# The last expert's output stays on chip: one-hot matmuls in place of its scatter-add to DRAM

## The chip, the cores and the metric

The kernel runs on one core of a Trainium2 chip. The core has TensorE (PE: matmuls and transposes, with its weight loads shown apart as PEld), VectorE (DVE), ScalarE (ACT), GpSimd (POOL), and SyncE (SP), which issues most of the DMAs. SBUF is the memory on the core, PSUM the memory that matmuls write to, DRAM lies outside. The metric is the device time of one execution in microseconds (us), as the median of several runs.

## The reference

One decoder layer over 512 tokens of width 1024, in float32. What matters here is its last third:

```
h = h + concat([ret, att]) @ w_out[i]
h = h + moe(rmsnorm(h, g_moe_norm[i]), ...)          # 32 experts, each token goes to 4
gate = jax.nn.sigmoid(h @ w_ple_gate[i])
h = h + rmsnorm(gate * (p[i] @ w_ple_proj[i]), g_ple_norm[i])
return rmsnorm(h, g_final)
```

In `moe`, a token's result is the sum over its four experts of (gate weight) x (expert output). An expert is an up projection to 2 x 1024 columns, a clamped SwiGLU, and a down projection to 1024 columns. The stage after it, called the epilogue below, multiplies `h` by `w_ple_gate` and needs the whole sum over the experts.

## The kernel before

**Sums in DRAM.** A DRAM tensor `acc` (512 x 1024) is first filled with the residual stream. The experts run one after another, sorted by their number of tokens. For each, POOL gathers its tokens' rows, PE runs the up and down projections, ACT multiplies the rows by the gate weights into a tile `y` (`gated`, line 928), and POOL adds them to `acc` with an indirect DMA that reads, adds and writes (`scatter`, line 933). After the last expert SP loads `acc` back in four tiles of 128 tokens, `h2[0]` to `h2[3]` (line 1165).

**Two kinds of experts.** The twenty larger ones (`BIG`, up to 96 rows) run on operands split into a high and a low part, three products each; the splits are lines 150 (ACT) and 151 (DVE). The twelve smaller ones (up to 64 rows) run in full float32 on unsplit weights; `pairs64` (line 861) computes two column halves side by side, so the output of such an expert is 128 x 512: rows 0 to 63 hold columns 0 to 511 of its up to 64 tokens, rows 64 to 127 the other columns of the same tokens. The last expert (number 31 in the order of work) is a small one.

**Buffers.** Weights arrive in 1 MB pieces in twelve tiles named `raw`. `raw_tile()` takes one, `free` lists those to be had, and `prefetch()` loads the next piece into one. Late in the kernel the same tiles serve other ends: `tmp` holds the input `p`, four halves of two tiles are `h2`, four of two others `proj`.

**Order of work at the end.** The code runs loop passes `e` = 0 to 32. Pass `e` does the up projection of expert `e` and the down projection of expert `e` - 1. At `e` = 31 a tile `last` is taken and left unused, and the activations of expert 31 are transposed (`act_t64`) before the down projection of expert 30. At `e` = 32 come the load and split of `p`, the loads of `w_ple_proj` and half of `w_ple_gate` (held back by a small ACT copy that reads the `y` of expert 30, line 221), the down projection of expert 31, its `gated` and its `scatter`. Then `project(0)` to `project(2)` multiply `p` by `w_ple_proj` for three of the four token tiles.

**A branch.** Line 1107 is a `tc.If` on whether an expert has more tokens than fit its rows. Each engine reads the flag and branches by itself; here the body is skipped. After the branch each engine waits until the work that it issued before is done, and then raises its semaphores by what the body would have added. The body uses most of PSUM, so the first PSUM users behind it wait for ACT's raise.

**Epilogue.** For each token tile `i`, `transposed(i)` (line 1176) transposes `h2[i]` on PE and splits it on ACT and DVE into `hh` and `hl`; `gate(i, c)` runs 24 matmuls for each column half `c`, a sigmoid and a sum of squares; `finish(i)` normalizes, adds and writes the output. They are called as transposed 0, project 3, gate 0 0, transposed 1, gate 1 0, gate 0 1, finish 0, gate 1 1, finish 1, and then transposed, two gates and finish for tiles 2 and 3.

**Who orders the instructions.** A scheduler orders the instructions of each engine by their place in the code and by when it computes them to be ready; an engine works through its list strictly in turn. So a later piece of code may stand earlier in an engine's list where the scheduler saw a gap.

Of the kernel before, what the change touches and what calls it, by code (L numbers as in the profile page):

```python
# [95 lines left out]
def hymba_kernel(ctx, tc, x, p, positions, rel_bias_table, g_mix_norm, w_in, b_in, ret_norm_g,  # L96
# [40 lines left out]
    def raw_tile(dt=F32):  # L137
        pl_ = free.pop(0)
        return pl_.tile([P, 2048], dt, name="raw"), pl_
# [77 lines left out]
    def prefetch(after=None):  # L217
        if free and state["next"] < min(len(pieces), state["limit"]):
            t, pl_ = raw_tile()
            if after is not None:  # L220
                nc.scalar.activation(t[:, 0:1], after[:, 0:1], AF.Copy)
            pieces[state["next"]](t)
            queue.append((t, pl_))
            state["next"] += 1

    def next_piece(parts=None, dst=None, more=True):
        t, pl_ = queue.pop(0)
        r = split(t, parts, dst)
        free.append(pl_)
        if more:  # L230
            prefetch()
        return r
# [590 lines left out]
    def act_t64(a):  # L823
        return transposed64(a, R.sb.tile([P, KD, 64], F32, name="aT64", bufs=1), 1.0 / ALPHA)
# [88 lines left out]
    def down(aT, piece, e):  # L913
        o = R.dn.tile([P, D], F32, name="dn")
        with tc.issue_after(R.up_end.ins):
            add_bias([o[:, 0:512], o[:, 512:D]], e, 1024, 512, start=True, stop=False)
        for f in range(4):
            wh, wl = piece(f)
            for kk in range(2):
                k = f * 2 + kk  # L920
                for a, w in ((aT[0], wh), (aT[1], wh), (aT[0], wl)):
                    for n in range(2):
                        nc.tensor.matmul(o[:, n * 512:(n + 1) * 512], lhsT=a[:, k, :],  # L923
                                         rhs=w[:, kk * 1024 + n * 512:kk * 1024 + (n + 1) * 512],
                                         start=False, stop=(k == KD - 1 and w is wl))
        return o

    def gated(o, gate):
        y = R.sb.tile([P, D], F32, name="y")
        nc.scalar.activation(y[:, 0:o.shape[1]], o, AF.Copy, scale=gate)  # L930
        return y

# [108 lines left out]
    with tc.issue_after(R.prep.ins):  # L1041
        ahead.append(next_piece())
    aT = None
    for e in range(E + 1):
        if e < E:
            def piece(k, e=e):
                if ahead:
                    return ahead.pop(0)
                with tc.issue_after(R.act.ins) if (e, k) == (1, 2) else nullcontext():
                    return next_piece()  # L1050

            if 0 < e < E - 2:
                static_gather(e + 2)
            h = up(xT, piece, e) if BIG[e] else up64(xT, e)
            a = act(h)
            if e == 0:
                read_slots()
                static_gather(2)
            if e + 1 < E:
                xT = (prep if BIG[e + 1] else prep64)(xe[(e + 1) % 2])  # L1060
        if e == E - 1:

            last = raw_tile()
            aT_last = act_t64(a)
        if e == E:
            tmp = raw_tile()
            p_sb = tmp[0][:, 0:D].rearrange("p (i d) -> p i d", i=NT)
            nc.sync.dma_start(out=p_sb, in_=p.rearrange("(i p) d -> p i d", p=P))
            state["limit"] = n_moe + 3
            for _ in range(3):  # L1070
                prefetch(after=y)
            ph, pl = halves(raw_tile(F32R)[0], 2)
            for i in range(NT):
                split_t(R.tp, p_sb[:, i, :], ph[:, :, i * P:(i + 1) * P], pl[:, :, i * P:(i + 1) * P], n=2)
            aT = aT_last
        if e > 0:
            big = BIG[e - 1]
            y = gated(down(aT, lambda f: next_piece(), e - 1) if big else down64(aT, e - 1), routes[e - 1][1])
            scatter(y, routes[e - 1][0], CAP if big else P, 1 if big else 2)
        if e < E - 1:  # L1080
            aT = act_t(a) if BIG[e] else act_t64(a)

    h2 = [t for _ in range(2) for t in raw_tile()[0].rearrange("p (a n) -> a p n", a=2)]
    proj = [t for _ in range(2) for t in raw_tile()[0].rearrange("p (a n) -> a p n", a=2)]
    state["limit"] = len(pieces)
    w_pr, *ws = [next_piece(more=False) for _ in range(3)]
# [20 lines left out]
    with tc.If(any_v > 0), ExitStack() as sx:  # L1107
# [9 lines left out]
        with tc.For_i(0, E, 1) as ev:  # L1117
# [4 lines left out]
            with tc.For_i(0, n_e, 1):  # L1122
# [33 lines left out]
                od = up_tile()  # L1156
                product(od, aTd, w_down, b_down, False)
                scatter(gated(od, gate), idx, P)


    ep2 = pool(ctx, "ep2", 2)
    mm = pool(ctx, "mm_e", 1, PSUM)
    tp = pool(ctx, "tp_e", 2, PSUM)
    for i in range(NT):
        ld = nc.sync.dma_start(out=h2[i], in_=acc[i * P:(i + 1) * P, :])
    with tc.issue_after(ld.ins):
        for _ in range(2):
            prefetch()
    g_ple = bcast(ep2, g_ple_norm[0], D, "g_ple", nc.sync)
    g_fin = bcast(ep2, g_final, D, "g_fin", nc.sync)  # L1170
    ws = [ws]
    free += [t[1] for t in (last, tmp, tf, tr)]
    hT = {}
    ss1 = {}

    def transposed(i):
        hT[i] = ep2.tile([P, KD, P], F32R, name="hh"), ep2.tile([P, KD, P], F32R, name="hl")
        split_t(tp, h2[i], *hT[i])

# [86 lines left out]
```

## Time and profile before

| | us |
|---|---|
| median of 3 runs | 1499.07 (1497.57 to 1502.2) |
| the profiled execution | 1498.92 |
| its span, first to last instruction | 1496.8 |
| PE busy | 1364.4 |
| DVE busy | 886.2 |
| ACT busy | 728.4 |
| POOL busy | 224.7 |

Busy times overlap, so they don't add up to the span. The profile shows the profiled execution alone, and its clock starts at the span's start. All that the change touches lies after 1335 us.

### The profile page before, as it was taken

How to read it: one execution, taken by the hardware profiler on the slowest of the kernel's cores; microseconds unless marked ns; L12 is line 12 of the kernel's file. 1: busy time of each engine (PE TensorE's matmuls, PEld its weight loads, DVE VectorE, ACT ScalarE, POOL GpSimd, SP SyncE). 2: the span in 40 equal slices, each digit the busy share in tenths (PEclk: the TensorE clock that was granted, in tenths of full speed). 3: DMA queues.
4: the chain of work that ended last, by engine and by line, in shares of the span. 5: the costliest groups of instructions: out<-in, count | busy, mean ns of one | idle time of the engine just before them, and what ended most of it. 6: DMA issues, size and time to landing. Idle time of an engine off the chain costs nothing. (4 is left out here: it accounts for less than half of the span.)

```text
span 1496.8 us, 17238 instructions
## 1 busy us (share of the span) xinstructions
PE 1364.4 (91%) x6208; PEld 939.3 (63%) x6209; DVE 886.2 (59%) x1052; ACT 728.4 (49%) x782; POOL 224.7 (15%) x230
## 2 busy tenths in 40 slices
PE   5998999588999999999999999999999999999785
PEld 4776777466676647656566647656567547675464
DVE  6635674767575627656466627656466627685256
ACT  5333543455464626544454626545455626664343
POOL 1203231472011100010100000010100100000023
PEclk9998999888999999999999999999999999999898
DMA  8432027677899999999999999999999999996601
GB/s 263 129 96 57 35 105 274 234 267 255 328 390 404 387 408 397 407 376 388 399 398 377 384 403 399 407 350 389 395 396 375 379 393 410 406 355 248 223 24 48
DMA packets 110428, 462.49 MB, mean 309 GB/s; under 512 B 10954, under 2 KB 29304, under 8 KB 77568
## 3 DMA queue, kind: packets, MB, share of 16 engines
q1 hardware_dynamic: 99584, 436.24, 74.5%
q0 software_dynamic: 10320, 24.51, 6.4%
q8 instruction: 50, 0.82, 0.2%
q10 hardware_dynamic: 432, 0.57, 0.1%
q14 instruction: 42, 0.34, 0.1%
HBM read 447.53 MB, written 18.99 MB: 312 GB/s over the span
## 5 line engine op out<-in xcount | busy, mean ns | idle before, releaser
L151 DVE TENSOR_TENSOR wl<-raw,wh 128x2048 fp32r<-128x2048 f32 (+2 forms) x267 | 584.1, 2229 | 125.2 <-ACT wh L150 124.3
L150 ACT ACTIVATE wh<-raw 128x2048 fp32r<-128x2048 f32 (+2 forms) x267 | 489.2, 1864 | 109.4 <-PE up L844 70.7
L844 PE MATMUL up<-wh,xTh 128*128 128x512 f32 x640 | 179.8, 403 | 13.1 <-ACT wh L150 11.6
L844 PE MATMUL up<-wl,xTh 128*128 128x512 f32 x640 | 179.3, 402 | 2.5 <-DVE wl L151 2.5
L844 PE MATMUL up<-wh,xTl 128*128 128x512 f32 x640 | 178.8, 401 | 0.9 <-DVE xTl L292 0.9
L861 PE MATMUL up<-raw,xTh 128*64 128x512 f32 x768 | 168.3, 594 | 0.0
L891 DVE TENSOR_SCALAR a<-up 128x512 f32<-128x512 f32 x52 | 34.0, 686 | 224.1 <-ACT sg L890 224.1
L844 PEld LDWEIGHTS up<-wh,xTh 128*128 128x128 f32 x640 | 120.4, 191 | 47.3 <-ACT wh L150 17.2
L844 PEld LDWEIGHTS up<-wl,xTh 128*128 128x128 f32 x640 | 120.7, 191 | 37.1 <-DVE wl L151 8.9
L844 PEld LDWEIGHTS up<-wh,xTl 128*128 128x128 f32 x640 | 121.7, 191 | 30.7 <-DVE xTl L292 1.6
L935 POOL DMA_INDIRECT acc<-y,slot_i x30 | 45.2, 1506 | 569.1 <-ACT y L930 497.4
L861 PEld LDWEIGHTS up<-raw,xTh 128*64 128x64 f32 x768 | 53.7, 137 | 104.6 <-issue 100.6
L923 PE MATMUL dn<-wl,aTh 128*128 128x512 f32 x320 | 102.6, 402 | 6.0 <-DVE wl L151 6.0
L890 ACT ACTIVATE sg<-up 128x512 f32<-128x512 f32 x52 | 28.9, 598 | 162.7 <-issue 148.2
L923 PE MATMUL dn<-wh,aTh 128*128 128x512 f32 x320 | 104.7, 409 | 0.1
L923 PE MATMUL dn<-wh,aTl 128*128 128x512 f32 x320 | 102.2, 401 | 0.0
L800 POOL DMA_INDIRECT xe<-xg,slot_i x30 | 42.9, 1429 | 370.8 <-PE tp L814 222.1
L861 PE MATMUL dn<-raw,aT 128*64 128x512 f32 x384 | 88.3, 598 | 0.0
L930 ACT ACTIVATE y<-dn,slots 128x1024 f32<-128x1024 f32 (+1 forms) x30 | 28.3, 944 | 102.7 <-PE dn L923 84.6
L923 PEld LDWEIGHTS dn<-wl,aTh 128*128 128x128 f32 x320 | 59.1, 189 | 22.8 <-DVE wl L151 10.0
L923 PEld LDWEIGHTS dn<-wh,aTl 128*128 128x128 f32 x320 | 61.2, 191 | 14.9
L923 PEld LDWEIGHTS dn<-wh,aTh 128*128 128x128 f32 x320 | 59.0, 191 | 17.3 <-ACT xTh L815 1.8
(338 smaller groups left out, 1577.2 us busy)
## 6 DMA issues: line engine op xcount, KB each, us to landing
raw<-in_w_up_dram SPq DMA_DIRECT2D x256, 1024.0 KB, 13.0
raw<-in_w_down_dram SPq DMA_DIRECT2D x128, 1024.0 KB, 12.3
raw<-in_w_in_dram SPq DMA_DIRECT2D x32, 256.0 KB, 4.9
raw<-in_w_out_dram SPq DMA_DIRECT2D x4, 1024.0 KB, 5.3
raw<-in_w_ple_gate_dram SPq DMA_DIRECT2D x4, 1024.0 KB, 11.4
raw<-in_w_in_dram SPq DMA_DIRECT2D x3, 1024.0 KB, 5.7
xt<-in_x_dram SPq DMA_DIRECT2D x4, 512.0 KB, 6.5
h<-in_x_dram POOLq DMA_DIRECT2D x4, 512.0 KB, 7.5
```

The costliest lines, as they stand in the source:

```text
L150: R.split_act = nc.scalar.activation(to(wh), src(raw), AF.Copy)
L151: R.split_dve = nc.vector.tensor_tensor(out=to(wl), in0=src(raw), in1=to(wh).bitcast(F32), op=ALU.subtract)
L800: return nc.gpsimd.indirect_dma_start(out=dst[0:n, 0:D // h], out_offset=None, in_=xg.rearrange("s (h d) -> (s h) d", h=h), in_offset=bass ...
L844: nc.tensor.matmul(h[n // 2][:, n % 2 * 512:n % 2 * 512 + 512], lhsT=a[:, k, :], rhs=w[:, n * 512:(n + 1) * 512], start=(k == 0 and a is x ...
L861: R.pair = nc.tensor.matmul(o[v * 64:v * 64 + 64, c:c + 512], lhsT=xT[:, k, :], rhs=w[:, v * n + c:v * n + c + 512], start=False, stop=las ...
L890: nc.scalar.activation(sg[:, cs], hv[:, :, 0], AF.Silu, scale=ALPHA)
L891: nc.vector.tensor_scalar(a[:, cs], hv[:, :, 1], LIMIT + 1.0, 1.0 - LIMIT, op0=ALU.min, op1=ALU.max)
L923: nc.tensor.matmul(o[:, n * 512:(n + 1) * 512], lhsT=a[:, k, :], rhs=w[:, kk * 1024 + n * 512:kk * 1024 + (n + 1) * 512], start=False, sto ...
L930: nc.scalar.activation(y[:, 0:o.shape[1]], o, AF.Copy, scale=gate)
L935: nc.gpsimd.indirect_dma_start(out=acc.rearrange("s (h d) -> (s h) d", h=h), out_offset=bass.IndirectOffsetOnAxis(ap=idx[0:n, :], axis=0), ...
```

## The change

The scatter of expert 31 is dropped. Its gated output `y` is written to a free part of `tmp`, and the read-back of `acc` (now `load_sums`) is issued before the down projection of expert 31, behind the scatter of expert 30. DVE builds a one-hot matrix `hot[:, i, :]` for each token tile: row r has a one in the column of the token to which row r of the expert belongs. `transposed(i)` then first multiplies this matrix with `y`, in two float32 matmuls of 64 rows (one for each column half), and DVE adds each product to `h2[i]` in place. `act_t64` of expert 31 now comes after the down projection of expert 30, `last` is gone, and the body of the `If`, which may add to `acc`, loads the sums again at its end.

```diff
-    def gated(o, gate):
-        y = R.sb.tile([P, D], F32, name="y")
+    def gated(o, gate, y=None):
+        if y is None:
+            y = R.sb.tile([P, D], F32, name="y")
         nc.scalar.activation(y[:, 0:o.shape[1]], o, AF.Copy, scale=gate)
         return y
...
+    def load_sums():
+        for i in range(NT):
+            R.sums = nc.sync.dma_start(out=h2[i], in_=acc[i * P:(i + 1) * P, :])
...
-        if e == E - 1:
-
-            last = raw_tile()
-            aT_last = act_t64(a)
...
-            aT = aT_last
+            h2 = [t for _ in range(2) for t in raw_tile()[0].rearrange("p (a n) -> a p n", a=2)]
+            load_sums()
+            hot = tmp[0][:, D:D + S].rearrange("p (i s) -> p i s", i=NT)
+            tok = small.tile([P, NT, 1], F32, name="tok", bufs=1)
+            r = RANK[E - 1]
+            nc.vector.tensor_scalar(tok, vb[:, :, 0:1], -1.0, slots[:, r, 0:1], op0=ALU.mult, op1=ALU.add)
+            for i in range(NT):
+                nc.vector.tensor_scalar(hot[:, i, :], iota, FAR, tok[:, i, :], op0=ALU.add, op1=ALU.is_equal)
         if e > 0:
             big = BIG[e - 1]
-            y = gated(down(aT, ...) if big else down64(aT, e - 1), routes[e - 1][1])
-            scatter(y, routes[e - 1][0], CAP if big else P, 1 if big else 2)
-        if e < E - 1:
+            y = gated(down(aT, ...) if big else down64(aT, e - 1), routes[e - 1][1],
+                      tmp[0][:, D + S:2 * D] if e == E else None)
+            if e < E:
+                scatter(y, routes[e - 1][0], CAP if big else P, 1 if big else 2)
+        if e < E:
             aT = act_t(a) if BIG[e] else act_t64(a)
-    h2 = [t for _ in range(2) for t in raw_tile()[0].rearrange("p (a n) -> a p n", a=2)]
...
                 scatter(gated(od, gate), idx, P)          # the last line of the If's body
+        load_sums()
...
-    for i in range(NT):
-        ld = nc.sync.dma_start(out=h2[i], in_=acc[i * P:(i + 1) * P, :])
-    with tc.issue_after(ld.ins):
-        for _ in range(2):
-            prefetch()
+    for _ in range(2):
+        prefetch()
...
     def transposed(i):
+        for v in range(2):
+            ps = mm.tile([P, 512], F32, name="mm", bufs=4)
+            rows, cs = slice(v * 64, v * 64 + 64), slice(v * 512, (v + 1) * 512)
+            nc.tensor.matmul(ps, lhsT=hot[rows, i, :], rhs=y[rows, :], start=True, stop=True)
+            nc.vector.tensor_tensor(out=h2[i][:, cs], in0=ps, in1=h2[i][:, cs], op=ALU.add)
         hT[i] = ep2.tile([P, KD, P], F32R, name="hh"), ep2.tile([P, KD, P], F32R, name="hl")
         split_t(tp, h2[i], *hT[i])
```

## Rows read from the trace of the kernel before

**Rows 1.** The page, part 1: busy us, share of the span, instructions.

```profile
PE 1364.4 (91%) x6208; PEld 939.3 (63%) x6209; DVE 886.2 (59%) x1052; ACT 728.4 (49%) x782; POOL 224.7 (15%) x230
```

**Rows 2.** Windows: length, busy us by engine, then PE clock, DMA share, GB/s.

```profile
1389.30:1400.10 10.80, 9.66 (x41) 3.41 (x41) 0.76 (x2) 2.66 (x7) 1.42 (x1) 1.00 0.74 247
...
1412.50:1418.85 6.35, 0.00 (x0) 0.00 (x1) 0.00 (x0) 1.02 (x1) 0.00 (x0) 0.76 0.98 358
1418.85:1425.20 6.35, 5.62 (x21) 4.39 (x21) 0.03 (x1) 1.57 (x3) 0.00 (x0) 0.71 0.68 261
...
1455.16:1460.20 5.04, 5.04 (x12) 3.98 (x13) 4.74 (x18) 1.52 (x5) 1.27 (x1) 0.51 0.27 104
```

**Rows 3.** Timeline of PE: start, duration, [idle before it <- what ended that].

```profile
1412.07 0.39 PE L309 MATMUL up<-wl,raw 128*128 128x512 f32 x1
1418.85 0.79 PE L307 MATMUL dn<-wh,raw 128*128 128x512 f32 x1 [6.39 <-ACTq L1107]
...
1423.43 1.03 PE L300 MATMUL tp<-cst,raw 128*128 128x128 f32 x8
1425.19 0.50 PE L307 MATMUL mm<-wh,hh 128*128 128x512 f32 x1 [0.73 <-ACT hh L291]
1425.91 0.50 PE L308 MATMUL mm<-wh,hl 128*128 128x512 f32 x1 [0.22 <-DVE hl L292]
...
1452.94 0.93 PE L307 MATMUL mm<-wh,hh 128*128 128x512 f32 x2 [1.83 <-ACT hh L291]
1455.16 0.80 PE L308 MATMUL mm<-wh,hl 128*128 128x512 f32 x1 [1.29 <-DVE hl L292]
```

**Rows 4.** Line 1107, the branch: count, duration ns, first and last start.

```profile
L1107 DVEq EVENT_SEMAPHORE  x2: 21/21/21, 1409.4 to 1409.5; - x2
...
L1107 ACTq EVENT_SEMAPHORE  x2: 17/17/17, 1418.8 to 1418.9; - x2
...
L1107 DVEq COMPARE_BRANCH  x1: 72/72/72, 1406.9 to 1406.9; - x1
...
L1107 ACTq COMPARE_BRANCH  x1: 50/50/50, 1413.0 to 1413.0; - x1
```

**Rows 5.** Instructions on `acc`, 1380 to 1440 us, and issue to landing.

```profile
L1165 SPq DMA_DIRECT2D raw<-acc x4: 345/386/807, 1406.4 to 1408.4; - x4
L935 POOL DMA_INDIRECT acc<-y,slot_i x2: 1416/1483/1550, 1390.7 to 1400.5; - x2
...
DMA to landing us min/median/max: 3.6/6.0/8.4
```

**Rows 6.** Timeline of PE, float32 matmuls of 64 rows in the attention.

```profile
139.74 2.09 PE L482 MATMUL s_ps<-akT,aqT 64*128 64x256 f32 x8
141.76 0.79 PE L315 MATMUL mm<-wh,act_l 128*128 128x512 f32 x1
...
142.60 1.13 PE L482 MATMUL s_ps<-akT,aqT 64*128 64x256 f32 x4
143.66 0.73 PE L315 MATMUL mm<-wh,act_l 128*128 128x512 f32 x2
```

**Rows 7.** Timeline of PE: 64-row bias matmuls between matmuls of 128 rows.

```profile
1344.99 1.10 PE L844 MATMUL up<-wl,xTh 128*128 128x512 f32 x4
1346.02 0.74 PE L831 MATMUL up<-bias,sel 64*128 64x512 f32 x4
1346.59 0.40 PE L831 MATMUL dn<-bias,sel 64*128 64x512 f32 x2
1346.92 0.74 PE L923 MATMUL dn<-wh,aTh 128*128 128x512 f32 x2
```

**Rows 8.** Line 751, a DVE addition of PSUM to SBUF in place.

```profile
L751 DVE TENSOR_TENSOR h<-mm,h x4: 691/692/692, 228.6 to 274.4; 128x512 f32<-128x512 f32 x4
```

**Rows 9.** Timeline of DVE at the third token tile.

```profile
1453.76 0.68 DVE L1192 TENSOR_TENSOR raw<-raw,sig 128x512 f32<-128x512 f32 x1
```

**Rows 10.** Timeline of PE at the start of expert 30's down projection.

```profile
1378.65 0.73 PE L923 MATMUL dn<-wl,aTh 128*128 128x512 f32 x2 [1.02 <-DVE wl L151]
```

More of the change, by code (lines that the diff above doesn't have):

```diff
@@ L1074, in hymba_kernel @@
                 split_t(R.tp, p_sb[:, i, :], ph[:, :, i * P:(i + 1) * P], pl[:, :, i * P:(i + 1) * P], n=2)
-            aT = aT_last
+            h2 = [t for _ in range(2) for t in raw_tile()[0].rearrange("p (a n) -> a p n", a=2)]
[6 more added lines that the diff above has]
+                nc.vector.tensor_scalar(hot[:, i, :], iota, FAR, tok[:, i, :], op0=ALU.add, op1=ALU.is_equal)
         if e > 0:
             big = BIG[e - 1]
-            y = gated(down(aT, lambda f: next_piece(), e - 1) if big else down64(aT, e - 1), routes[e - 1][1])
-            scatter(y, routes[e - 1][0], CAP if big else P, 1 if big else 2)
-        if e < E - 1:
+            y = gated(down(aT, lambda f: next_piece(), e - 1) if big else down64(aT, e - 1), routes[e - 1][1],
+                      tmp[0][:, D + S:2 * D] if e == E else None)
+            if e < E:
+                scatter(y, routes[e - 1][0], CAP if big else P, 1 if big else 2)
+        if e < E:
             aT = act_t(a) if BIG[e] else act_t64(a)
-    h2 = [t for _ in range(2) for t in raw_tile()[0].rearrange("p (a n) -> a p n", a=2)]
     proj = [t for _ in range(2) for t in raw_tile()[0].rearrange("p (a n) -> a p n", a=2)]
@@ L1171, in hymba_kernel @@
     ws = [ws]
-    free += [t[1] for t in (last, tmp, tf, tr)]
+    free += [t[1] for t in (tf, tr)]
     hT = {}
```

## The prediction

> **What bounds the kernel now.** I first read the page: PE is busy for 1364.4 of 1496.8 us [rows 1], so PE sets the pace and the question is where it stands idle. The change is confined to the end, so next I read PE's timeline there, then the instructions on `acc`, and last the branch. The reader should see three things.
>
> First, what PE waits for after the down projection of expert 31. It goes on with `project(0)` to `project(2)`, which need no expert's output, until 1412.07 + 0.39 = 1412.46. Then it idles for 6.39 us, and ACT's branch ends that idle time, no DMA [rows 3]. It then runs `project(3)`, which also needs no expert, and the first transposes of `h2` start at 1423.43 [rows 3].
>
> Second, where the scatter and the read-back stand against that. The scatter of expert 31 is issued at 1400.5, the four loads from 1406.4 to 1408.4, and none of these DMAs takes over 8.4 us from issue to landing [rows 5]. So the last tile is there by 1408.4 + 8.4 = 1416.8 at the latest, 6.6 us before even the first tile is touched, and 2 us before ACT lets PE go at all.
>
> Third, ACT's branch itself. It executes at 1413.0 in 0.05 us, but ACT's next instruction comes at 1418.8, 5.8 us later [rows 4]. In this stretch the DMA engines are 0.98 busy with the read-back and two weight loads [rows 2]. DVE's branch came at 1406.9 and its next instruction at 1409.4 [rows 4]: 2.5 us at most, for it also finished a split meanwhile. [...]
>
> **The change part by part.** The sum is made against the profiled execution, 1498.92 us, which stands 0.15 us below the median of 1499.07; I add the result to the median.
>
> *Scatter removed, read-back moved ahead: 0.* Both are covered by `project` and the branch, as above. From the issue of the scatter to the last landing they take 1416.8 - 1400.5 = 16.3 us; were ACT's branch free and PE at `h2` 5 us earlier, at 1418.4, the cover would still hold. The loads now wait on SP for expert 30's scatter, issued at 1390.7 and landed at most 8.4 us later, at 1399.1 [rows 5]. Behind them in SP's list stand SP's branch, then two loads of `w_ple_gate` and the two norm vectors. Those weights are used after two gates have run, some 20 us after the branch, so I cost that queue at nothing.
>
> *The branch: -1.1.* [...] Below: DVE's 2.5 in place of 5.8, a gain of 3.3. Above: 0, the DMA engines being full already. I take a third of the gain, since about half of the traffic goes and its moment is uncertain.
>
> [...]
>
> *The transposes of expert 31 moved behind expert 30's down projection: 0.* In front of it they gave nothing away, because that projection then waits for a DVE split anyway, 1.02 us at 1378.65 [rows 10]; that wait also swallows what is saved. Behind it they may cost their own time, half of the 1.03 us that eight transposes take [rows 3]. Bounds 0 and +0.5.
>
> *Building the one-hot matrices: 0.* Five small DVE instructions; from 1389.3 to 1400.1 DVE is busy for 0.76 of 10.8 us [rows 2]. Without that cover they would cost at most five times an addition of 512 columns, 3.5 us [rows 8].
>
> *Two float32 matmuls per token tile: 1.6 us a tile.* The trace has no such matmul of 64 x 512. The nearest are those of line 482, 64 x 256. A float32 matmul shows as two instructions; four of them go from 142.60 to 143.66 at full clock [rows 6]; less 0.2 us for the change of shape (below) that is 0.215 each, and 0.43 for twice the columns. Two matmuls are four instructions: 1.72 us end to end. If the two, which use different halves of the array's rows, run fully side by side, it is 0.86. That they can: eight instructions from 139.74 to 141.76 [rows 6] are two such streams, in 2.02 us at half clock where one by one they would need 3.4. Here the instructions come in pairs of one half, so only the inner two can overlap: three steps, 1.29. To it I add the change between 64 and 128 rows: the four from 1344.99 on follow each other at (1.10 - 0.40) / 3 = 0.233, the first bias matmul comes 0.10 late, and the six of them, in three pairs, take 0.20 more than three such steps [rows 7]. Together 0.3, so 1.6 (bounds 0.86 and 2.0).
>
> [...]
>
> *Two additions per tile on DVE: 0.69 us each* [rows 8]. They stand between matmul and transposes. The first half of the tile is added some 0.2 us after its matmul (the handing over from DVE to PE at 1425.91 has this size [rows 3]), so it is ready at 0.86 + 0.2 + 0.69 = 1.75 us while PE is done at 1.29: 0.45 idle. The second half is ready 0.69 later, four transposes take 0.5: 0.2 more. So 0.65 us of PE idle where nothing fills it.
>
> Now tile by tile. *Tile 0:* `project(3)` is ready and fills the wait, and it can also fill the 0.73 + 0.22 us that PE now waits after the transposes [rows 3]: 1.6 - 0.95 = +0.65. The half clock after the branch (0.71 on average, [rows 2]) strikes the new work instead of `project(3)`, so it costs nothing twice. *Tile 1:* 1.6 + 0.65 = +2.25. *Tile 2:* PE already idles 1.83 + 1.29 us here [rows 3], because `hl` stands behind `finish(0)` and line 1192 [rows 9] in DVE's list; the matmuls fit into that, but two more additions come ahead of `hl`: +1.4. *Tile 3:* +2.25. Sum 6.55; with the branch 5.45. That gives 1499.07 + 5.45 = **1504.5 us**. Tiles at 0.86 and 2.0 us, the moved transposes and the branch at their ends give +1.0 and +8.3 (the idle terms kept, tile 2 unchanged).
>
> **The rivals.** About 0.3%, 4.5 us, is what a measurement of this kernel can tell from no change: 1494.6 to 1503.6.
>
> *A, the forecast:* the new instructions stand in PE's list where the code has them.
>
> *B, pulled ahead.* The one-hot matmuls need neither `h2` nor the weights, so the scheduler may put tile 1's beside tile 0's, and tile 3's into PE's idle 3.1 us at tile 2. Then tile 1 costs 1.6, tile 3 nothing: 0.65 + 1.6 + 1.4 - 1.1 = +2.55, **1501.6**. For it: such fillings are how the lists are made. Against it: in the scheduler's reckoning PE may have no gap there.
>
> [...]
>
> [...]
>
> [...]
>
> **How the numbers follow.** A 0.43, of which 0.08 end below 1503.6; B 0.31; C 0.16, of which 0.10 end below 1494.6; D 0.10. Faster 0.10; same 0.08 + 0.31 + 0.06 = 0.45; slower 0.35 + 0.10 = 0.45. The time is A's. The range, 1496 to 1510, leaves out D and 0.10 of C; A's own is 1500 to 1507.4.
>
> **What would show it.** Right: the read-back is issued near 1399 and PE still stands idle until ACT's branch; each tile has four float32 instructions of 64 rows in 1.3 us at full clock; PE idles under a microsecond before the transposes of tiles 1 and 3. Wrong: PE ends `project(2)` well before 1412, or ACT's branch is over well before 1417; either moves all that follows. The forecast also falls if the clock stays full at tile 2.

## The result and the profile after

| | before | after |
|---|---|---|
| median of the runs timed together, us | 1502.16 | 1510.59 |
| ratio, 95% interval | | 1.0056 [1.0041, 1.007] |
| the profiled execution, us | 1498.92 | 1510.74 |
| its span, us | 1496.8 | 1509.0 |

The change makes the kernel 8.4 us (0.56%) slower. The forecast was slower by 5.45 us, and its range ended at 1510: the direction is right, the size too small, the time just beyond the range. Of the 6.1 us between the forecast of 1504.5 and the 1510.59, 3.1 are the median of the kernel before, 1502.16 here and 1499.07 in the forecast, and 3.0 are the change. One of the six executions of after took 4702.75 us, and the ratio leaves it out. Page of after, part 1 (the answer to [rows 1]):

```profile
PE 1374.1 (91%) x6224; PEld 942.5 (62%) x6225; DVE 892.1 (59%) x1065; ACT 729.3 (48%) x782; POOL 224.0 (15%) x229
```

PE has 16 instructions more, and is busy 9.7 us longer. Up to the end of expert 30 the changed part of the kernel has not begun to matter to PE, and yet the profile of after is already 3.5 us late there; such a shift appears between any two executions (the same point lies between 1389.4 and 1396.3 in the runs of this study). So from here on I compare the **stretch** from expert 31's first bias matmul (1390.44 before, 1393.91 after) to the end of the span: 106.4 us before, 115.1 after, +8.7. That is the measured loss (8.4 by the medians). A stretch is that of one execution; how well it repeats can be seen in e2 below, which differs from before by one scatter that costs nothing: each of its five windows agrees with the one below within 0.1 us. A ratio also holds what varies ahead of the stretch, so the two need not agree: in e7 the stretch is 3.8 us longer than before, and the ratio stands for 1.0.

The windows view cuts the stretch at the last matmul of four gates: up to the end of `gate(0, 0)`; tile 1 (to `gate(1, 1)`); tile 2; tile 3; and what comes after PE's last matmul. Columns: length, then busy us of PE, PEld, DVE, ACT and POOL, then PE's granted clock, DMA share, GB/s. Before:

```profile
1390.44:1431.54 41.10, 31.22 (x123) 20.16 (x124) 9.49 (x9) 12.74 (x17) 2.97 (x2) 0.88 0.64 217
1431.54:1450.23 18.69, 18.16 (x83) 14.37 (x81) 10.54 (x17) 9.82 (x14) 3.82 (x3) 1.00 0.00 0
1450.23:1468.39 18.16, 15.04 (x59) 11.47 (x57) 12.78 (x37) 7.61 (x18) 7.62 (x6) 0.81 0.15 59
1468.39:1481.47 13.08, 12.67 (x81) 10.94 (x78) 9.82 (x26) 5.89 (x14) 4.19 (x4) 1.00 0.07 26
1481.47:1496.83 15.36, 0.00 (x1) 0.00 (x0) 8.58 (x24) 3.39 (x10) 4.86 (x5) 0.58 0.12 46
```

After, the same five cuts:

```profile
1393.91:1436.48 42.57, 33.47 (x127) 21.06 (x127) 15.37 (x13) 17.74 (x20) 1.42 (x1) 0.84 0.60 205
1436.48:1456.73 20.25, 19.33 (x87) 14.58 (x86) 7.60 (x18) 4.99 (x11) 3.88 (x3) 1.00 0.00 0
1456.73:1479.28 22.55, 18.95 (x64) 12.93 (x63) 14.25 (x40) 7.72 (x18) 7.58 (x6) 0.77 0.12 47
1479.28:1494.46 15.18, 14.05 (x82) 11.35 (x82) 11.05 (x27) 5.99 (x14) 5.05 (x4) 1.00 0.09 35
1494.46:1508.98 14.52, 0.00 (x1) 0.00 (x0) 7.70 (x24) 3.40 (x10) 3.98 (x5) 0.62 0.10 37
```

Half of the loss, 22.55 - 18.16 = 4.39 us, lies at tile 2, and 3.9 of those are PE *busy* longer, not idle longer. Over the four windows with gates PE is busy 2.25 + 1.17 + 3.91 + 1.38 = 8.71 us longer, as much as the stretch grows. Read that with the clock beside it: 0.77 over the window. PE's timeline of after tells what is in it:

```profile
1421.83 2.08 PE L1189 MATMUL mm<-raw 64*128 64x512 f32 x4 [5.79 <-ACTq L1118]
1424.68 1.11 PE L300 MATMUL tp<-cst,raw 128*128 128x128 f32 x4 [0.78 <-DVE raw L1190]
...
1436.41 1.13 PE L1189 MATMUL mm<-raw 64*128 64x512 f32 x4
1438.32 1.25 PE L300 MATMUL tp<-cst,raw 128*128 128x128 f32 x8 [0.78 <-DVE raw L1190]
...
1456.66 1.13 PE L1189 MATMUL mm<-raw 64*128 64x512 f32 x4
1461.39 1.97 PE L300 MATMUL tp<-cst,raw 128*128 128x128 f32 x8 [3.60 <-DVE raw L1190]
1463.19 1.22 PE L307 MATMUL mm<-wh,hh 128*128 128x512 f32 x2
1464.35 2.07 PE L1189 MATMUL mm<-raw 64*128 64x512 f32 x2
...
1479.20 1.12 PE L1189 MATMUL mm<-raw 64*128 64x512 f32 x2
1480.26 0.66 PE L300 MATMUL tp<-cst,raw 128*128 128x128 f32 x4
```

Four groups of one-hot matmuls were expected, and there are five. Tile 3's were split: two of its four instructions stand inside the first gate of tile 2 (1464.35), where PE runs at half clock (0.50 in the windows below), and take 2.07 us instead of 1.12. Ahead of tile 2's transposes PE waits 3.60 us for the addition on DVE. DVE's timeline shows why it is late:

```profile
1458.19 0.67 DVE L254 SCALAR_TENSOR_TENSOR rs_v<-ss_f 128x1 f32<-128x1 f32 x1 [0.79 <-ACT raw L1224]
...
1459.99 0.68 DVE L1206 TENSOR_TENSOR raw<-raw,sig 128x512 f32<-128x512 f32 x1
1460.60 0.14 DVE L271 TENSOR_SCALAR rs_t<-rs_t 128x1 f32<-128x1 f32 x1
1460.66 0.68 DVE L1190 TENSOR_TENSOR raw<-mm,raw 128x512 f32<-128x512 f32 x1
```

The product is there at 1457.8, but the addition stands behind the second half of `finish(0)` (line 254 and what follows) and a `sig` multiplication. PE's clock behind the two long waits, in windows of after (columns as above):

```profile
1421.91:1425.91 4.00, 3.22 (x9) 1.65 (x10) 1.29 (x2) 0.08 (x1) 0.00 (x0) 0.50 0.70 242
1425.91:1429.91 4.00, 4.00 (x13) 3.18 (x13) 2.34 (x2) 2.81 (x3) 0.00 (x0) 0.53 0.08 27
1461.91:1465.91 4.00, 4.00 (x11) 2.05 (x9) 3.19 (x13) 1.80 (x3) 0.86 (x1) 0.50 0.16 62
1465.91:1469.91 4.00, 4.00 (x9) 2.81 (x9) 2.71 (x7) 1.24 (x4) 0.44 (x1) 0.50 0.19 73
1469.91:1473.91 4.00, 4.00 (x17) 3.24 (x16) 3.35 (x10) 0.15 (x2) 2.09 (x2) 0.91 0.00 0
```

Busy time times (1 - clock) is my estimate of what the clock cost: 1.6 + 1.9 = 3.5 behind the branch and 2.0 + 2.0 + 0.4 = 4.4 behind tile 2, 7.9 us. Before, the same product from [rows 2] is 5.62 x 0.29 + 5.04 x 0.49 = 4.1. So by this estimate about 3.8 of the 8.71 us are the clock. The other 4.9 are about what the one-hot matmuls of four tiles take with the change of shape (1.1 to 1.3 us a tile, worked out below).

Of the things that were to change nothing, two lines. The branch (now line 1118; the answer to [rows 4]) and the read-back (now line 1048; to [rows 5]):

```profile
L1118 ACTq EVENT_SEMAPHORE  x2: 17/17/17, 1421.8 to 1421.8; - x2
...
L1118 ACTq COMPARE_BRANCH  x1: 50/50/50, 1416.6 to 1416.6; - x1
```

```profile
L1048 SPq DMA_DIRECT2D raw<-acc x4: 339/400/429, 1402.5 to 1403.8; - x4
```

The read-back is issued at 1402.5, 3.5 us of shift beyond the 1399 that was forecast. ACT's branch takes 5.2 us in place of 5.8, with the DMA engines busy for 0.65 of it and no longer 0.99. The difference tells little: with the read-back moved, ACT's branch takes 5.4 us in e1, 4.0 in e7 and 5.3 in e12. The prediction's -1.1 us for the branch takes it that less traffic on the DMA engines shortens it. DVE's next instruction comes 2.5 us behind its branch in both kernels, with the DMA engines busy for 0.70 of it before and for the whole of it after; a split on DVE fills 2.43 and 2.50 us of that, so the branch by itself can't be read there. That traffic sets the length of the branch is not shown.

### The profile page after: what moved, and what is told of

Its sections match the earlier page's. It is cut to its first block, busy times and chain, and to the rows that moved or that the text cites. A ratio compares the mean times of both kernels' runs of the same rounds, so it can differ in the third digit from the quotient of the medians.

```text
span 1509.0 us, 17281 instructions
## 1 busy us (share of the span) xinstructions
PE 1374.1 (91%) x6224; PEld 942.5 (62%) x6225; DVE 892.1 (59%) x1065; ACT 729.3 (48%) x782; POOL 224.0 (15%) x229
## 5 line engine op out<-in xcount | busy, mean ns | idle before, releaser
L150 ACT ACTIVATE wh<-raw 128x2048 fp32r<-128x2048 f32 (+2 forms) x267 | 489.7, 1865 | 108.4 <-PE up L844 67.0
L923 PE MATMUL dn<-wh,aTh 128*128 128x512 f32 x320 | 104.3, 407 | 0.1
```

The lines of the kernel that those rows point to most:

```text
L150: R.split_act = nc.scalar.activation(to(wh), src(raw), AF.Copy)
```

## The experiments

Sixteen kernels. "Stretch" is that of the profiled execution of each; ratios are to the kernel before. The computation is left incomplete in e1, e2, e3, e10, e11 and e16: there the last expert's rows, or those of some tiles, are missing.

### What moving the read-back gives, without the one-hot work

**e1** leaves the five lines of the one-hot loop out of `transposed`, **e2** is the kernel before less one scatter:

```diff
 # e1, in after's transposed(i)
-        for v in range(2):
-            ps = mm.tile([P, 512], F32, name="mm", bufs=4)
-            ...
 # e2, in before
-            scatter(y, ...)
+            if e < E:
+                scatter(y, ...)
```

> The changed kernel without the one-hot matmuls and the additions (the last expert's output is left out of the sum); the earlier read-back and all else stay. Read: ratio to before, and the stretch from the first bias matmul of expert 31's down projection to the end (before 106.4 us, changed 115.1). Theory 'work in the epilogue': all that was lost is the one-hot work, so the stretch falls back to 105 to 107 and the ratio is 1.000 within 0.002. Rival 'moved read-back': the loads now stand ahead of the branch in SP's list and delay what follows; then the stretch stays above 112 and the ratio above 1.003.

Measured: 0.9965 [0.9951, 0.9979], stretch 101.0: below what either theory had.

> The kernel before without expert 31's scatter (its output is left out of the sum), the read-back where it was. Theory 'hidden': the scatter stands beside project and ACT's branch, so the stretch stays at 106.4 within 1 us and the ratio is 1.000 within 0.002. Rival 'scatter on the path': the stretch falls by the 4.5 us that the scatter took to land, or more, and the ratio is below 0.998.

Measured: 0.9996 [0.9987, 1.0006], stretch 106.4. The scatter and its cover are as forecast: worth nothing. But e1, where the scatter is gone, the read-back moved and the one-hot work left out, is 5.4 us shorter than before. A part of the cause is in its PE timeline:

```profile
1416.41 1.07 PE L300 MATMUL tp<-cst,raw 128*128 128x128 f32 x8 [0.45 <-PEq L1118]
1421.97 0.80 PE L307 MATMUL dn<-wh,raw 128*128 128x512 f32 x1 [4.50 <-ACTq L1118]
```

The transposes of tile 0 now stand ahead of `project(3)` in PE's list and run while PE would only wait for ACT's branch; before, they came behind it [rows 3]. No transfer got shorter on the path: an *order* changed, and the window up to `gate(0, 0)` fell from 41.10 to 38.72. And tile 2 took 15.64 us instead of 18.16:

```profile
1450.73:1466.37 15.64, 12.57 (x58) 9.76 (x57) 12.44 (x36) 7.59 (x18) 7.39 (x6) 1.00 0.10 38
```

PE's idle time there is the same as before, 3.07 against 3.12 us; the clock stayed at 1.00, where it was 0.81.

**e6** is the kernel before, with that order alone:

```diff
+    with tc.issue_after(R.tr.ins):          # R.tr: the last transpose
         project(mm.tile([P, D], F32, name="dn"), (3,))
```

> The kernel before with one change: PE's transposes of token tile 0 are put ahead of project(3) in PE's list; scatter, read-back and all else stay. Theory 'the gain of the first experiment is a place in PE's list': the transposes need no PSUM of the branch's body, so they run while ACT branches, and the stretch falls from 106.4 to 103.5 to 104.6 with the scatter still in place. Rival 'the gain comes from the missing scatter and the earlier read-back': the stretch stays at 106 to 107.

Measured: 0.9986 [0.9976, 0.9996], stretch 104.0. PE's timeline of e6 has the transposes where e1 has them:

```profile
1416.79 1.06 PE L300 MATMUL tp<-cst,raw 128*128 128x128 f32 x8 [0.45 <-PEq L1107]
```

The order by itself gives 2.4 us, without any of the change. e1 has 3 us more: 1.55 of it is tile 2 again, which took 17.19 us here at a clock of 0.90, and 1.44 is tile 1 (19.62 us against 18.18). This order explains neither.

### What the one-hot work costs, by kind and by tile

After against e1: 115.1 - 101.0 = 14.1 us, where the prediction's terms sum to 6.55. **e11** keeps the matmuls and drops the additions; **e10**, **e3** and **e16** leave the one-hot loop out for tile 0, tile 2, and tiles 1 and 3:

```diff
 # e11
-            nc.vector.tensor_tensor(out=h2[i][:, cs], in0=ps, in1=h2[i][:, cs], op=ALU.add)
 # e10, e3, e16
-        for v in range(2):
+        for v in range(2 if i != 0 else 0):      # e3: i != 2;  e16: i % 2 == 0
```

> The kernel after with all its one-hot matmuls, but none of the additions: the products stay unused in PSUM and the last expert's rows are missing from the sums. Theory (the matmuls cost their own 1.1 to 1.6 us a tile and hold tile 0's transposes behind ACT's branch; the rest of the 14.1 us is the additions, for which PE waits and behind which the splits queue): stretch 106 to 108, in place of 115.1 with the additions and 101.0 without either. Rival (it is the matmuls: the change of shape and the half clock that follows): stretch 112 to 115, ratio over 1.003.

Measured: 1.0012 [1.0001, 1.0024], stretch 109.0: between the two theories. The matmuls, with what they hold up, are 8.0 of the 14.1 us, the additions 6.1.

> The kernel after without the one-hot matmuls and the additions of token tile 0 (the last expert's rows are missing from that tile's sums); tiles 1 to 3 keep theirs. Theory (tile 0's matmuls need PSUM that the body of the If uses, so they and the transposes behind them can't run under ACT's branch; without them the transposes run there and the branch hides them): the first gate matmul comes at 33 us of the stretch in place of 36.8, and the stretch falls from 115.1 to 110.5 to 112. Rival (a tile costs its matmuls and one wait for its addition, wherever it stands): first gate matmul at 34.5 to 35.5, stretch 112.7 to 113.7.

Measured: 1.0006 [0.9995, 1.0016], stretch 108.8. First half right: tile 0's transposes are under ACT's branch again, 0.45 us behind PE's own as in e1, and the first gate matmul comes at 32.9 us of the stretch. The stretch fell by 6.3, more than either theory said: up to tile 2 the gain is 3.9, and then tile 2, whose code is that of after, takes 19.80 us in place of 22.55:

```profile
1450.56:1470.36 19.80, 16.22 (x64) 11.38 (x63) 14.16 (x39) 7.83 (x18) 7.59 (x6) 0.91 0.14 54
```

Same wait (3.58), same instructions; PE's clock came back earlier, 0.91 on average against 0.77. Tile 3's pair stands in the first gate of tile 2 here too, and most of it runs at full clock (0.60 from 1457.75 to 1458.75, then 1.00):

```profile
1458.15 1.30 PE L1189 MATMUL mm<-raw 64*128 64x512 f32 x2
```

> The changed kernel without the matmuls and additions of token tile 2 alone (that tile lacks the last expert's output). Theory 'DVE queue': tile 2 costs 4.4 of the 8.7 us, since its additions stand behind the work of finish(0) on DVE; the stretch falls from 115.1 to about 110.7. Rival 'each tile costs its matmuls': tile 2 costs what tiles 0, 1 and 3 do, about 2, and the stretch is about 113.

Measured: 1.0006 [0.9994, 1.0017], stretch 109.4, tile 2 16.96 us long. The stretch fell by 5.7 us, more than the theory's 4.4 and far from the rival's 2.

> The kernel after without the one-hot matmuls and additions of token tiles 1 and 3 (the last expert's rows are missing from those tiles); tiles 0 and 2 keep theirs. Theory (these two tiles cost what the milestones of the new kernel show, 1.5 and 2.1 us): the stretch falls from 115.1 to 111 to 112, ratio 1.0025 to 1.0035. The prediction's terms (2.25 each) give 110.6. Rival (leaving out any tile also reorders what stands behind it, as leaving out tile 0 gave 6.3 us): stretch 107 to 109.5, ratio under 1.0015.

Measured: 1.0015 [1.0003, 1.0028], stretch 108.4: the rival, though not for its reason. Tiles 1 and 3 give back 2.06 and 2.11 in their own windows, almost what the prediction had. The rest is at tile 2:

```profile
1454.63:1473.69 19.06, 15.38 (x62) 11.11 (x63) 13.56 (x38) 7.87 (x18) 7.58 (x6) 0.91 0.15 56
```

The wait of 3.59 us is still there and tile 2's own matmuls too; what is gone is tile 3's pair in the middle of the half-clock stretch, and 22.55 - 19.06 = 3.5 us with it. The pair alone need not be the cause, for e10 has it in the same place and is 2.75 us shorter than after at tile 2. By busy time times (1 - clock) the low clock at tile 2 costs 18.95 x 0.23 = 4.4 us in after, 1.5 in e10 and 1.4 in e16: by this estimate some 3 us of either gain are the clock.

So single tiles give back 6.3 (0), 5.7 (2) and 6.6 (1 and 3), 18.6 in all where the sum is 14.1: each also shortens the half clock behind tile 2 (mean clock of that window 0.91, 0.90 and 0.91, against 0.77), and that can be gained only once.

### Moving the additions, and moving what waits for them

**e4** and **e5** call `transposed(2)` ahead of `finish(0)`, and no longer behind `finish(1)`, in after and in before:

```diff
     gate(0, 1)
+    transposed(2)
     finish(0)
...
-        transposed(i)
+        if i > 2:
+            transposed(i)
```

> The changed kernel with transposed(2) (its matmuls, additions, transposes and splits) called ahead of finish(0) instead of after finish(1); nothing is left out. Theory 'DVE queue': PE's 3.6 us wait for tile 2's additions shrinks to the 0.8 of tile 1, and the slow clock after it goes too; the stretch falls by 5 to 8 us, to 107 to 110. Rival 'each tile costs its matmuls': only PE's amount of work counts, and the stretch stays at 114 to 116.

Measured: 1.0018 [1.0008, 1.0028], stretch 110.3. The wait at tile 2 fell to 0.29, and the next one appeared:

```profile
1476.36 1.97 PE L300 MATMUL tp<-cst,raw 128*128 128x128 f32 x8 [4.45 <-DVE raw L1190]
```

Tile 3's addition now stands behind `finish(1)`.

> The kernel before with transposed(2) called ahead of finish(0); nothing is left out. Theory 'tile 2 is bound by the order on ACT and DVE': PE's waits of 1.83 and 1.29 us at tile 2 and the slow clock after them go, and the stretch from expert 31's first bias matmul to the end falls from 106.4 to 101 to 103, ratio 0.996 to 0.998. Rival 'DVE has too much to do': the work of finish is only pushed back and meets the end; stretch 105 or more.

Measured: 0.9983 [0.9974, 0.9993], stretch 104.3: the same in the kernel before, tile 2 without idle time and then 4.64 us for `hh` at tile 3.

**e7** puts all eight additions ahead of the branch (and once more at the end of its body), **e8** is e7 with `transposed(2)` early, **e12** puts tiles 0 and 1 there and tiles 2 and 3 behind `transposed(1)` and `gate(1, 0)`, and calls `transposed(2)` and `transposed(3)` ahead of the two finishes:

```diff
+    def add_last(i, ps):                 # e12; e7 and e8: all four tiles in one loop
+        for v in range(2):
+            rows, cs = slice(v * 64, v * 64 + 64), slice(v * 512, (v + 1) * 512)
+            nc.tensor.matmul(ps[v], lhsT=hot[rows, i, :], rhs=y[rows, :], start=True, stop=True)
+            nc.vector.tensor_tensor(out=h2[i][:, cs], in0=ps[v], in1=h2[i][:, cs], op=ALU.add)
+    ...                                  # called ahead of the If, into up_tile()
     any_v = nc.values_load(any_blk[0:1, 0:1], min_val=0, max_val=NT)
```

> The changed kernel with the one-hot matmuls and additions of all four tiles issued ahead of the branch, behind project(2), and repeated in its body; the split of the last weights is kept behind the branch. Nothing is left out. Theory 'cover': PE idles 5.8 us and DVE 11 us there, so the eight matmuls (4.5 us) and eight additions (5.5 us) hide, and the stretch falls from 115.1 to 101 to 104, below the 106.4 of before; ratio 0.996 to 0.999. Rival 'DVE's own branch': the additions hold it back, PE waits for it in turn, and the stretch stays at 106 to 109.

Measured: 1.0007 [0.9997, 1.0016], stretch 110.2. The rival's mechanism held, a little beyond its range of 106 to 109. In e7's PE timeline and its branch lines:

```profile
1424.88 1.97 PE L300 MATMUL tp<-cst,raw 128*128 128x128 f32 x8 [3.60 <-DVEq L1128]
```

```profile
L1128 DVEq EVENT_SEMAPHORE  x2: 21/21/21, 1424.8 to 1424.9; - x2
...
L1128 DVEq COMPARE_BRANCH  x1: 72/72/72, 1421.9 to 1421.9; - x1
```

DVE reaches its branch only at 1421.9, behind the additions, and PE waits for DVE's branch instead of ACT's.

> The kernel of the run before (additions ahead of the branch) and transposed(2) called ahead of finish(0). If both theories hold the two gains add: stretch 96 to 100, ratio 0.993 to 0.996. If tile 2's gain is only pushed back, it is that of the run before.

Measured: 1.0006 [0.9995, 1.0018], stretch 109.4; it is e7 with the wait of 4.87 us moved to tile 3.

> The kernel after with its one-hot additions moved: those of tiles 0 and 1 ahead of the branch, beside the projections (and once more in the skipped body), those of tiles 2 and 3 behind the transposes of tile 1 and the first gate of tile 1; the transposes of tiles 2 and 3 come ahead of finish(0) and finish(1), and a weight split of DVE and ACT comes behind the splits of tile 0. Nothing of the computation changes. Theory (the additions cost only where they stand between a tile's matmul and its transposes, or hold up DVE's list): stretch 101 to 104, ratio 0.996 to 0.999. Rival (the four additions ahead of the branch make DVE's branch late, as in the run with all eight there): PE waits for DVE's branch again, stretch 106 to 110, ratio 1.000 to 1.002.

Measured: 1.0000 [0.9991, 1.0008], stretch 106.8. DVE's branch is late again, by less (PE waits 3.86 us, to 30.0 of the stretch), and no other wait is left; the last gate matmul ends at 86.8 us of the stretch, 4.3 ahead of before, but the end comes 20.0 us behind it and not 15.4. Of the versions of the change that compute everything it has the shortest stretch. By its ratio it is level with the kernel before, and so are e7 and e8: the three intervals overlap, and all contain 1.

### The order alone, the last finishes, and PE's idle time

**e9** is the kernel before with the order of e6 and e12 (transposes of tile 0 first, tiles 2 and 3 ahead of the finishes) and nothing of the change. **e14** is e9 with `finish(3)` and then `finish(2)` behind the last gate. **e15** is e14 with five useless float32 matmuls in PE's wait for ACT's branch. **e13** is after with fourteen useless matmuls in PE's wait at tile 2.

```diff
 # e9, e14, e15 (besides the lines of e6)
     gate(0, 1)
+    transposed(2)
     finish(0)
     gate(1, 1)
+    transposed(3)
     finish(1)
     ...                                  # no transposed(i) in the loop behind; e14: its finishes behind the loop
 # e15, ahead of transposed(0); fill is a PSUM tile that nobody reads
+    for _ in range(5):
+        f = nc.tensor.matmul(fill, lhsT=h2[0][:, 0:P], rhs=h2[0][:, 0:512], start=True, stop=True)
 # e13, in after's transposed(i), behind the additions
+        if i == 2:
+            for _ in range(14):
+                nc.tensor.matmul(fill, lhsT=hT[1][0][:, 0, :], rhs=kslice(ws[0][0][0], 0), start=True, stop=True)
```

> The kernel before, with the order of three pieces changed and none of the change in it: PE's transposes of tile 0 stand ahead of project(3), and the transposes and splits of tiles 2 and 3 come ahead of finish(0) and finish(1). Nothing of the computation changes. Theory (what the one-hot kernel gains is the order alone, and each of the three pieces gives some of it): the stretch from expert 31's first bias matmul to the end falls from 106.4 to 97 to 101 us, ratio 0.994 to 0.997, and no wait of over 1 us for DVE or ACT is left ahead of the gates of tiles 2 and 3. Rival (the finishes, pushed back, become late themselves and take the gain at the end): stretch 102 to 104, ratio 0.998 to 0.9995, as each piece gave alone.

Measured: 0.9978 [0.9969, 0.9987], stretch 102.7: the rival. Gates run without a gap, the last matmul ends at 82.8 us of the stretch, and 19.9 us follow it. Two finishes' worth of DVE is left there: 12.23 us busy against 8.58 before.

> e9_before_early with finish(2) called behind the last gate and finish(3), in place of between the gates of tiles 2 and 3. Theory (e9's last gate matmul came 8.3 us earlier than in the kernel before, but the last gate's sigmoid stood in ACT's list behind a step of finish(2), which gave back 4.5 us): the last gate matmul stays at 82.8 us of the stretch and the end comes at 96.5 to 99, ratio 0.9935 to 0.9965. Rival (two finishes behind the last gate share DVE, which is the bound there in either order): end at 101.5 to 104, ratio 0.997 to 0.999.

Measured: 0.9968 [0.9956, 0.998], stretch 102.0. The rival's time again: 19.2 us behind the last matmul here, 19.9 in e9. That DVE is the bound there, as the rival has it, is not shown: it is busy for 11.87 of the 19.2 us.

> e14_finish2_late with five useless float32 matmuls of 128x512 (0.86 us each, 4.3 us) in PE's list ahead of the transposes of tile 0, in the time in which ACT branches; their product is read by nobody. Theory (PE's half clock behind the branch follows from its idle time there; it strikes project(3) and costs 2 us): PE runs project(3) at full clock and the stretch is 1.5 to 2.2 us shorter than that of e14. Rival (the idle time is not the cause, or the rest of the chain starts with ACT and not with PE): the same as e14 within 0.5 us, or longer.

Measured: 0.9954 [0.9937, 0.9971], stretch 99.0, 3.0 shorter than e14. The useless matmuls fill PE's wait, which is 4.61 us long in e14, up to the transposes:

```profile
1416.09 4.53 PE L1224 MATMUL tp<-raw 128*128 128x512 f32 x10 [0.45 <-PEq L1107]
```

Windows over `project(3)` of tile 3, from its first matmul to the first of the gate, e14 and then e15:

```profile
1421.78:1426.68 4.90, 4.90 (x13) 3.85 (x14) 1.29 (x2) 1.08 (x2) 0.00 (x0) 0.55 0.63 247
```

```profile
1421.73:1424.59 2.86, 2.86 (x13) 2.36 (x14) 1.29 (x2) 1.09 (x2) 0.00 (x0) 1.00 1.01 307
```

Same twelve matmuls, same start; with PE kept busy ahead of them they run at full clock (1.00 against 0.55) and take 2.04 us less (busy time times (1 - clock) would be 2.2). One more microsecond comes back at tile 1, where a wait of 0.65 + 0.80 becomes 0.46. By its median this is the fastest version here, and it beats both kernels; its interval overlaps that of e14.

> The kernel after with 14 useless matmuls of 128x512 (0.233 us each at full clock, 3.3 us) in PE's list between the one-hot matmuls and the transposes of tile 2, where PE waits 3.6 us; their product is read by nobody. Theory (the half clock behind tile 2 follows from PE's idle time there and costs 4.3 us): PE stays at full clock through the gates of tile 2, the stretch falls from 115.1 to 110 to 112 us, ratio 1.002 to 1.0035. Rival (the clock falls for another reason, or the time is lost to DVE's queue alone): PE's clock is 0.5 behind tile 2 as before, stretch 114.5 to 116, ratio 1.005 to 1.007.

Measured: 1.0073 [1.0053, 1.0093], stretch 115.3. My theory fell in its result. PE's timeline of e13:

```profile
1455.88 1.13 PE L1189 MATMUL mm<-raw 64*128 64x512 f32 x4
1456.94 3.52 PE L1194 MATMUL mm<-wh,hh 128*128 128x512 f32 x14
1460.67 1.32 PE L300 MATMUL tp<-cst,raw 128*128 128x128 f32 x8 [0.20 <-DVE rs_y L272]
1464.01 0.73 PE L307 MATMUL mm<-wh,hh 128*128 128x512 f32 x2 [2.01 <-ACT hh L291]
1464.67 1.12 PE L1189 MATMUL mm<-raw 64*128 64x512 f32 x2
1466.26 0.63 PE L308 MATMUL mm<-wh,hl 128*128 128x512 f32 x1 [0.47 <-DVE hl L292]
```

The wait was filled, PE stayed at full clock through it (1.00 from 1456.73 to 1466) and tile 3's pair took 1.12 and not 2.07. But then it waited 2.01 + 0.47 us for `hh`, which stands behind the output step of `finish(0)` in ACT's list, and `hl`, behind a step of `finish(1)` in DVE's, and the clock fell behind *that* wait (0.63 us a matmul from 1466.26 on, up to 1469.7; 0.57 on average from 1466 to 1470). What was saved on the clock was lost as idle time; the stretch is the same within 0.3 us.

## Why the prediction was wrong

By its own terms, against the windows above:

| term of the sum | predicted, us | measured, us |
|---|---|---|
| branch and tile 0 | -1.1 + 0.65 = -0.45 | +1.47 |
| tile 1 | +2.25 | +1.56 |
| tile 2 | +1.4 | +4.39 |
| tile 3 | +2.25 | +2.10 |
| behind the last matmul | 0 | -0.84 |
| sum | +5.45 | +8.68 |

**What held.** The scatter is hidden (e2). The moved transposes of expert 31 cost nothing: from the last matmul of its up projection to its bias matmul it is 17.25 us before and 17.26 after. An addition takes 0.68 us, and PE's wait for one where nothing fills it is 0.78, forecast as 0.65. The one-hot matmuls are a little cheaper than 1.6. Four instructions at full clock take 1.06 us (e13, 1455.88 to 1456.94), less than the 1.29 I chose. A pair of one half takes the same 1.06 (after, 1479.20 to 1480.26), so the two halves ran side by side for their whole length: two steps and not three. A step is the forecast's 0.43 (in e15 an instruction of 512 columns and 128 rows takes that); the other 0.2 of the 1.06 I put down to the change of shape, and with 0.09 ahead of the group and 0.10 behind it, that makes an estimate of 0.4 in all, near the forecast's 0.3. At tile 1 PE is busy 1.17 us longer and idle 0.39, since the wait of 0.78 comes in part in place of waits for the splits. Of the branch's 1.1 us 0.6 came (5.8 us before, 5.2 after). No run shows the term itself, that less traffic shortens the branch, which was the author's estimate: with the read-back moved ACT's branch took from 4.0 (e7) to 5.4 us (e1).

**What failed: the clock, which the sum has at nothing.** Its terms are work and waits. By busy time times (1 - clock), the estimate above, the low clock costs 7.9 us in after and 4.1 in before, and these 3.8 us are more than the 3.2 by which the sum is short. Half of them falls at tile 2 and half behind the branch.

**The step that failed first: tile 2, +1.4.** I wrote that the matmuls fit into PE's idle time there, and that two more additions come ahead of `hl`. The second is true. The first is not: the matmuls ran ahead of the wait (1456.66 to 1457.79), and PE then stood idle for 3.60 us, where before it had 3.12 in all. Of the +4.39 us, 0.5 is that wait, 1.9 the clock (by the estimate, 4.4 us against 2.5), and the other 2.0 about the work of two groups, for tile 3 was missing as well. Rival B saw that its matmuls might be pulled ahead and priced that as a gain, into the idle time; A had them where the code has them. They were pulled ahead by half, into the gate *behind* the wait, where PE runs at half clock (0.50): 2.07 us there, and 1.1 for the other pair at tile 3. Splitting them cost the side-by-side running as well: all four together take 1.13 at tiles 1 and 2. e16 has tile 2 alone, with its wait of 3.59 us, at 19.06 against 18.16 before: +0.9, near the +1.4 by luck, because PE's clock is 0.91 there and 0.81 before.

**The second: "the half clock after the branch strikes the new work instead of `project(3)`, so it costs nothing twice".** It struck both. After has two windows at 0.50 and 0.53 behind the branch, 7.2 busy us, where before has 5.62 at 0.71 [rows 2]: by the estimate 3.5 us lost and not 1.6. The one-hot matmuls ran for 2.08 us at half clock (0.50), PE waited for the addition (0.78 us), and `project(3)` ran at half clock up to 1429.7 (0.50 from 1424.68 on). e15 shows what that clock is worth: with PE busy ahead of `project(3)`, it takes 2.86 us at 1.00 instead of 4.90 at 0.55 (e14).

**A gain that was not seen, and was lost again.** "Scatter removed, read-back moved ahead: 0" looked only at the transfers. With the read-back moved, tile 0's transposes also went ahead of `project(3)`, under the branch. That order alone is worth 2.4 us (e6), and e1 as a whole 5.4, of which 2.5 lie at tile 2, where the clock stayed at 1.00. The one-hot matmuls of tile 0 take the order's gain back, for their PSUM tiles come behind the branch and the transposes come behind them (e10: +3.9 at tile 0). Rival C stood for a faster ending by another way, that the wait at tile 2 goes. Rival D, that additions get stuck behind `finish` on DVE at tiles 1 and 3 too and PE falls to half clock, had the right mechanism in the wrong places: it is tile 2 where it happens, and tile 3 once tile 2 is moved (e4).

**What stays open.** Why PE's clock stayed at 1.00 at tile 2 of e1 and fell to 0.90 in e6 and 0.81 before, behind 3.0 to 3.1 us of idle time in all three, and why the low clock behind tile 2 lasted shorter in e10 and e16 than in after. The runs show what it cost, not what decides it. That filling PE's idle time ahead of a stretch raised the clock in it is shown at the branch only (0.55 behind 4.61 us of idle time in e14, 1.00 in e15); at tile 2 e13 could not hold the rest still.

## What to carry to other kernels

A step that leaves a queue also changes the order of everything behind it, so price a move by the lists of instructions that it reorders and not by its transfers alone: here the scatter was worth nothing (e2) and one changed order 2.4 us (e6), and the kernel before gets 4.4 by order alone, without the change (e14, 0.9968). New work on PE cost three things here: its own time (1.1 to 1.3 us a tile), the wait for whoever finishes it (0.78 us at tile 1, 3.60 at tile 2), and PE's clock behind that wait (at tile 2 an estimated 4.4 us in place of 2.5). Work behind the wait for the branch ran at a low clock wherever it was read, but for e15: 0.50 in before, after, e1, e3, e9, e10, e11 and e13, 0.55 in e14, 0.56 to 0.59 in e12, and 1.00 in e15. Work put *into* a wait cost next to nothing in both cases here: it gave 3 us of the stretch back at the branch (e15) and none at tile 2 (e13, 115.3 against 115.1). And when a wait is removed, name the next instruction that stands behind the same work: three times in this study it took back about half of the gain or more (4.0 of 8.8 us in e4, 4.4 of 6.4 in e5, 4.5 of 8.3 in e9).

## What the runs showed of the hardware

- Two float32 matmuls of 64 rows, one on rows 0 to 63 of its operands and one on rows 64 to 127, took as long as one: 1.06 us for four instructions of 512 columns (e13, 1455.88 to 1456.94) and 1.06 for two (after, 1479.20 to 1480.26), at a clock of 1.00 in both. At the change between 64 and 128 rows, the group at 1436.41 (after) starts 0.09 us later than the rhythm of the gate matmuls (0.233 us each) would have put it. Behind such a group the first matmul of 128 rows holds the next one back by 0.34 us in place of 0.233 (e13), and within it the steps are 0.53 us where an instruction of 512 columns and 128 rows takes 0.43 (e15). Together that gives an estimate of 0.4 us for there and back.
- From the branch, whose body is skipped, to its next instruction ACT took 5.8 us before, 5.2 after, 5.4 in e1, 4.0 in e7 and 5.3 in e12, and DVE 2.5 in before, after and e1, 2.9 in e7 and 3.1 in e12. In before and after a split was running on DVE for 2.43 and 2.50 us of that; what sets ACT's was not isolated.
- A chain of twelve matmuls took PE 4.90 us at a mean clock of 0.55 behind 4.61 us of idle time (e14), and 2.86 at 1.00 when ten useless instructions had kept PE busy for 4.5 us ahead of it (e15): work that nobody reads made the stretch 3.0 us shorter.
